# A decoder trunk's residual stream and FFN products kept token by token: tokens stationary, 512 weight columns moving

## The chip, the cores and the metric

The kernel runs on one core of a Trainium2 chip. The metric is the device time of one execution in microseconds; three runs were timed, and their median counts. The profile is of one further execution, read by the hardware profiler. TensorE (PE) multiplies matrices; VectorE (DVE), ScalarE (ACT) and GpSimd (POOL) work on elements; SyncE's queue (SP) issues the loads of the weights. Every engine works through its own list of instructions in order.

## The reference

Two layers act on x, 256 tokens of 1024 features. Each adds half of an FFN, a mixer, a cross-attention (xattn) into 256 memory tokens, and half of a second FFN. The mixer of layer 0 is a state-space head group with pooled channels; that of layer 1 is windowed attention with learned sinks. All is in float32.

```python
def rms_norm(x, gain):
    return x * lax.rsqrt(jnp.mean(x * x, axis=-1, keepdims=True) + EPS) * gain

def swiglu(h, wi, wo):                       # wi 1024 x 5632, wo 2816 x 1024
    gate, up = jnp.split(h @ wi, 2, axis=-1)
    return (jax.nn.silu(gate) * up) @ wo

for i in range(2):
    x = x + 0.5 * swiglu(rms_norm(x, ffn1_norm[i]), ffn1_wi[i], ffn1_wo[i])
    h = rms_norm(x, mix_norm[i])
    x = x + (ssd_pool_mixer(h, ...) if i == 0 else swa_sink_attention(h, ...))
    x = x + memory_cross_attention(rms_norm(x, xattn_norm[i]), mem_k, mem_v, xattn_wq[i], ...)
    x = x + 0.5 * swiglu(rms_norm(x, ffn2_norm[i]), ffn2_wi[i], ffn2_wo[i])
```

## The kernel before

A float32 product is done as three products of rounded parts (`mm3`, lines 165 to 167): hi by hi, lo by hi, hi by lo. Weights come in chunks, up to 1 MB each, through SP's queue into `raw`; ScalarE casts the hi part (`whi`, line 92) and VectorE subtracts the lo part (`wlo`, line 93), in pieces of 128 x 1024, five of which are held at a time. Taking a chunk starts the load and the split of the next one.

The residual stream `x` lies feature by feature: eight k tiles of 128 features by 256 tokens. In the FFN's two products, the q and output projections, a 128 x 128 tile of weights stays in TensorE and the 256 tokens move through it: a product is 128x256. Only the memory's and attention's keys and values (`token_mm`, line 936) and the last FFN's second product (`ffn_last`, line 509) have the tokens stay and 512 weight columns move: a product is 128x512.

When tile m of x is final, `x_ready` writes its scaled input for the next block at once: `h_hi` by ScalarE (274), `h_lo` by VectorE (275), its square (257) and the running sum `acc` (258). Behind the eighth tile, four passes of a product with ones add up the squares over the partitions (`stat`, 220), a chain of eleven small VectorE instructions makes rstd (`var` to `rcol`, 191 to 204 and 223), and another product spreads it over the partitions (`diag`, `rbc`, 228 and 237). What needs rstd is deferred until then, so the first products of a block run on the unscaled input. In the FFN, VectorE scales gate and up (`gu`, 441), ScalarE takes Silu (444), and `a_hi`, `a_lo` (446, 447) are the input of the second product.

TensorE's list is written in the order of the code. Small products, transposes among them, are put into it some tiles after the point that defers them: `LAGS` is the table, and `tick` counts four split products of 256 columns as one tile. On the other engines, instructions follow in the order of the program that a scheduler keeps.

The blocks in their order, with the layer as a number: FFN1_0, the memory's keys and values, mixer, xattn0, FFN2_0, FFN1_1, attention, xattn1, FFN2_1. "Border" below is the place in TensorE's list where one block's first large product follows the last of the block before.

Of the kernel before, what the change touches and what calls it, by code (L numbers as in the profile page):

```python
# [8 lines left out]
F32 = mybir.dt.float32  # L9
# [7 lines left out]
P = 128  # L17
# [9 lines left out]
# When the tensor engine's small products are issued: tiles (4 split products of 256 columns)  # L27
# after the point that defers them.
LAGS = {
    "sums": 6, "spread": 10, "first_keep": 2, "first_sums": 3, "first_spread": 7, "memT": 16, "kT": 12,  # L30
    "steps": 2, "decays": 14, "seg": [19, 21, 23, 24, 26, 49, 52, 54],
    "weigh": [25, 26, 27, 29, 31, 51, 57, 59], "cbt": 8, "pool": 9, "group_sums": 6, "group_spread": 15,
    "last": 2, "keys": 6, "xsT": [9, 13, 17, 20], "heads": [13, 16, 19, 22, 29, 34, 40, 46],
    "x_norm": [8, 11, 15, 17], "x_scores": [11, 12, 16, 20], "x_weights": [12, 12, 16, 22],
# [5 lines left out]
    "x_sums": 6, "a_sums": 4, "a_spread": 8, "m_sums": 4, "m_spread": 7,  # L40
# [4 lines left out]
# columns of the constant array  # L45
# [17 lines left out]
class Trunk:  # L63
# [11 lines left out]
    # ------------------------------------------------------------ helpers  # L75
# [11 lines left out]
    def split(self, raw, a, b):  # L87
        """hi + lo parts of [P, a, b] weights."""
        nc = self.nc
        hi = self.wp.tile([P, a, b], F32R, tag="whi", name="whi")  # L90
        lo = self.wp.tile([P, a, b], F32R, tag="wlo", name="wlo")
        nc.scalar.copy(hi, raw)  # L92
        nc.vector.tensor_tensor(out=lo, in0=raw, in1=hi.bitcast(F32), op=ALU.subtract)  # L93
        return hi, lo

    # The weights' chunks are listed in the order of their use; taking one starts the next one's
    # load and split.
    def plan(self, src, ka, cols, step):
        self.chunks.append((src, ka, cols, step))
# [5 lines left out]
    def load_chunk(self, by_part=False):  # L105
# [3 lines left out]
        src = src.rearrange("(k p) c -> p k c", p=P)  # L109
        if by_part:  # L110
            loads = [lambda k=slice(u, min(u + step, ka)): self.nc.sync.dma_start(
                out=raw[:, k, :], in_=src[:, k, :]) for u in range(0, ka, step)]
        else:
            self.nc.sync.dma_start(out=raw, in_=src)
# [18 lines left out]
    # Small products of the tensor engine are put between the large ones, some tiles after what  # L133
    # they wait for was started (LAGS).
# [4 lines left out]
    def tick(self, n=1):  # L139
# [3 lines left out]
        if self.count < 4:  # L143
            return
        self.count -= 4
        self.now += 1
# [98 lines left out]
    def warm(self, func):  # L245
        """has the scalar engine's table for func loaded."""
# [13 lines left out]
    def x_ready(self, m, gain):  # L260
        """x tile m is final for this block: its part of the next block's scaled input and norm."""
        nc = self.nc
        if gain is None:
            return
        xm = self.x[:, m, :]
        if m == 0:
            self.acc = self.sp.tile([P, NT], F32, tag="acc", name="acc")
        if gain[2]:
            self.square_into(self.acc, xm, m == 0)
            if m == KT - 1:  # L270
                self.normalised(gain)
            return
        g = self.col(gain[0], 8 * gain[1] + m)
        nc.scalar.activation(self.h_hi[:, m, :], xm, AF.Identity, scale=g)
        nc.vector.scalar_tensor_tensor(out=self.h_lo[:, m, :], in0=xm, scalar=g,
                                       in1=self.h_hi[:, m, :].bitcast(F32), op0=ALU.mult, op1=ALU.subtract)
        self.square_into(self.acc, xm, m == 0)
        if m == KT - 1:
            name = {"xattn_norm": "x_", "mix_norm": "a_"}.get(gain[0], "")
            self.block_rstd(self.acc, name, gain[0] != "xattn_norm")  # L280

    def block_rstd(self, acc, name="", wide=True):
# [3 lines left out]
        def done():  # L286
# [3 lines left out]
        self.R, self.RB = self.rstd(acc, D, self.sp, "rbx", name, done, wide)  # L290
# [7 lines left out]
    def normalised(self, gain):  # L298
        """the next block's input, normalised before its products."""
        nc = self.nc  # L300

        def scale():
            for m in range(KT):
                t = self.sp.tile([P, NT], F32, tag="xn", name="xn", bufs=3)
                nc.vector.scalar_tensor_tensor(out=t, in0=self.x[:, m, :],
                                               scalar=self.col(gain[0], 8 * gain[1] + m), in1=rb,
                                               op0=ALU.mult, op1=ALU.mult)
# [1023 lines left out]
```

## Time and profile before

| | |
|---|---|
| three runs | 1199.64, 1200.95, 1201.68 us |
| median | 1200.95 us |
| span of the profiled execution | 1198.2 us |
| the profiled execution's own time | not recorded beside the span; it is a fourth execution, not one of the three |
| TensorE busy | 1185.6 us, 99% |
| VectorE, ScalarE, GpSimd busy | 826.8, 666.6, 27.7 us |
| moved by DMA | 204.00 MB, 170 GB/s in the mean |

A busy time counts an instruction from its start to its end. Products of TensorE overlap: one of 256 columns lasts 0.28 us, but the next starts long before that. How long one holds up the next is read from starts that follow each other. In the list of groups, the idle time after the bar is that of the engine just before such an instruction, with what ended it.

### The profile page before, as it was taken

The page shows a single profiled execution, that of the slowest core. Times are in us where ns is not written, and L with a number is a line of the kernel's source. Part 1 is how long each engine was busy: PE and PEld are TensorE (multiplying, and loading weights), DVE is VectorE, ACT ScalarE, POOL GpSimd, SP SyncE. Part 2 cuts the span into 40 slices and gives each one's busy share as a digit, 9 for nine tenths or more (in the row PEclk, how much of TensorE's full clock was granted, in tenths as well). Part 3 has the DMA queues.
Part 4 walks back from the last instruction along what each step waited for, and adds up shares of the span by engine and source line. Part 5 has one row for each costly group of instructions (what it writes and reads, how often), then busy time and mean ns, then how long its engine had stood idle before and what let it go on. Part 6 is the DMA issues. An engine that isn't in the chain of part 4 may idle for free.

```text
span 1198.2 us, 22743 instructions
## 1 busy us (share of the span) xinstructions
PE 1185.6 (99%) x9351; PEld 1147.7 (96%) x9351; DVE 826.8 (69%) x1558; ACT 666.6 (56%) x1109; POOL 27.7 (2%) x45
## 2 busy tenths in 40 slices
PE   8999999999999999999999999999999999999998
PEld 8999999889999999999999999999988999999987
DVE  6767655879888786766655766665797877676642
ACT  7446444876775566544544544544478665554541
POOL 2000000000000000000000000000410000000000
PEclk9999999999999999999999999999999999999999
DMA  8564655554455534556465556455622434554651
GB/s 293 177 211 142 207 186 166 198 175 143 141 176 176 185 107 141 175 178 200 149 208 185 175 176 204 157 191 187 208 97 85 162 121 141 176 185 167 210 186 61
DMA packets 178231, 204.00 MB, mean 170 GB/s; under 512 B 4630, under 2 KB 162592, under 8 KB 178128
## 3 DMA queue, kind: packets, MB, share of 16 engines
q1 hardware_dynamic: 176512, 201.93, 51.2%
q8 instruction: 73, 1.20, 0.4%
q10 hardware_dynamic: 1040, 0.32, 0.1%
q0 software_dynamic: 576, 0.31, 0.1%
q14 instruction: 30, 0.25, 0.1%
HBM read 201.50 MB, written 1.05 MB: 169 GB/s over the span
## 4 chain that ended last, share of the span: by engine, by line
PE 96%; DVE 1%; ACT 1%; DMA 0%; issue 0%; SPq 0%; DVEq 0%
PE mmb L165 27%; PE mmb L166 26%; PE mmb L167 26%; PE mmb L509 5%; PE mmb L936 5%; PE oT L1219 0%; DMA xn<-in_x_dram 0%; PE pT L1207 0%; PE yps L651 0%; DVE wlo L93 0%; PE rbc L237 0%; ACT s L1188 0%; PE sc L1164 0%; PE pT L1015 0%; PE seg L552 0%
## 5 line engine op out<-in xcount | busy, mean ns | idle before, releaser
L93 DVE TENSOR_TENSOR wlo<-raw,whi 128x1024 fp32r<-128x1024 f32 (+1 forms) x385 | 462.4, 1204 | 182.1 <-ACT whi L92 180.9
L92 ACT CAST whi<-raw 128x1024 fp32r<-128x1024 f32 (+1 forms) x385 | 396.9, 1035 | 255.3 <-PE mmb L166 197.5
L165 PE MATMUL mmb<-h_hi,whi 128*128 128x256 f32 x1824 | 521.3, 286 | 1.4 <-ACT whi L92 1.4
L167 PE MATMUL mmb<-h_hi,wlo 128*128 128x256 f32 x1824 | 517.2, 284 | 1.7 <-DVE wlo L93 1.7
L166 PE MATMUL mmb<-h_lo,whi 128*128 128x256 f32 x1824 | 517.0, 283 | 0.0
L165 PEld LDWEIGHTS mmb<-h_hi,whi 128*128 128x128 f32 x1824 | 350.7, 192 | 4.5 <-issue 2.4
L167 PEld LDWEIGHTS mmb<-h_hi,wlo 128*128 128x128 f32 x1824 | 350.6, 192 | 2.1 <-DVE wlo L93 2.1
L166 PEld LDWEIGHTS mmb<-h_lo,whi 128*128 128x128 f32 x1824 | 350.8, 192 | 0.1
L167 PE MATMUL mmb<-a_hi,wlo 128*128 128x256 f32 x528 | 149.2, 283 | 0.0
L165 PE MATMUL mmb<-a_hi,whi 128*128 128x256 f32 x528 | 149.0, 282 | 0.0
L166 PE MATMUL mmb<-a_lo,whi 128*128 128x256 f32 x528 | 148.7, 282 | 0.0
L441 DVE TENSOR_TENSOR gu<-mmb,rb 128x512 f32<-128x512 f32 x88 | 60.2, 687 | 74.7 <-PE mmb L167 72.3
L444 ACT ACTIVATE s<-gu 128x256 f32<-128x256 f32 x88 | 36.4, 417 | 135.2 <-DVE gu L441 134.8
L166 PEld LDWEIGHTS mmb<-a_lo,whi 128*128 128x128 f32 x528 | 100.7, 191 | 0.0
L165 PEld LDWEIGHTS mmb<-a_hi,whi 128*128 128x128 f32 x528 | 100.7, 191 | 0.0
L167 PEld LDWEIGHTS mmb<-a_hi,wlo 128*128 128x128 f32 x528 | 100.6, 191 | 0.0
L446 ACT CAST a_hi<-s 128x256 fp32r<-128x256 f32 x88 | 35.3, 404 | 37.5 <-DVE s L445 37.5
L445 DVE TENSOR_TENSOR s<-s,gu 128x256 f32<-128x256 f32 x88 | 36.8, 421 | 19.8 <-ACT s L444 19.7
L447 DVE TENSOR_TENSOR a_lo<-s,a_hi 128x256 fp32r<-128x256 f32 x88 | 36.8, 421 | 17.0 <-ACT a_hi L446 17.0
L166 PE MATMUL mmb<-o_lo,whi 128*128 128x256 f32 x128 | 36.4, 284 | 2.0 <-DVE o_lo L1034 2.0
L165 PE MATMUL mmb<-o_hi,whi 128*128 128x256 f32 x128 | 36.6, 286 | 0.0
L167 PE MATMUL mmb<-o_hi,wlo 128*128 128x256 f32 x128 | 36.2, 283 | 0.0
(321 smaller groups left out, 1483.4 us busy)
## 6 DMA issues: line engine op xcount, KB each, us to landing
raw<-in_ffn_wi_dram SPq DMA_DIRECT2D x86, 1024.0 KB, 5.2
raw<-in_ffn_wo_dram SPq DMA_DIRECT2D x34, 1024.0 KB, 5.3
raw<-in_ssd_in_proj_dram SPq DMA_DIRECT2D x14, 1024.0 KB, 5.2
raw<-in_ffn_wo_dram SPq DMA_DIRECT2D x12, 768.0 KB, 4.6
raw<-in_mem_wkv_dram SPq DMA_DIRECT2D x8, 1024.0 KB, 5.2
raw<-in_even_out_proj_dram SPq DMA_DIRECT2D x8, 1024.0 KB, 5.1
raw<-in_xattn_wq_dram SPq DMA_DIRECT2D x8, 1024.0 KB, 5.1
raw<-in_xattn_wo_dram SPq DMA_DIRECT2D x8, 1024.0 KB, 5.0
```

The costliest lines, as they stand in the source:

```text
L92: nc.scalar.copy(hi, raw)
L93: nc.vector.tensor_tensor(out=lo, in0=raw, in1=hi.bitcast(F32), op=ALU.subtract)
L165: mm(ps, lhsT=wh, rhs=xh, start=start, stop=False, skip_group_check=True)
L166: mm(ps, lhsT=wh, rhs=xl, start=False, stop=False, skip_group_check=True)
L167: mm(ps, lhsT=wl, rhs=xh, start=False, stop=stop, skip_group_check=True)
L441: nc.vector.tensor_tensor(out=gu, in0=bank.rearrange("p (a n) -> p a n", a=2), in1=self.RB[:, None, :].to_broadcast([P, 2, NT]), op=ALU.mult)
L444: nc.scalar.activation(s, gu[:, 0, :], AF.Silu)
L445: nc.vector.tensor_tensor(out=s, in0=s, in1=gu[:, 1, :], op=ALU.mult)
L446: nc.scalar.copy(a_hi[:, f, :], s)
L447: nc.vector.tensor_tensor(out=a_lo[:, f, :], in0=s, in1=a_hi[:, f, :].bitcast(F32), op=ALU.subtract)
L509: nc.tensor.matmul(banks[b], lhsT=l[:, f, tok], rhs=r, start=f == 0 and i == 0, stop=f == NFF - 1 and i == 2)
L936: self.nc.tensor.matmul(ps, lhsT=l[:, f, tok], rhs=r, start=f == 0 and i == 0, stop=f == KT - 1 and i == 2)
```

## The change

`x` now lies token by token: two blocks of 128 tokens by 1024 features. `tok3` keeps 128 tokens in TensorE and moves 512 weight columns; both FFN products, the mixer's, xattn's and attention's output projections use it. q projections and the mixer's input projections still move 256 tokens.

`add_rows` adds 128 x 512 of a result to x, and ScalarE squares that and sums it by token at once (`square`). `half_ready` runs when 512 features of x are final: it puts two transposes for each of the four k tiles into TensorE's list (`turn_in`), behind which `put` writes `h_hi` and `h_lo` from PSUM; behind the second half, `token_rstd` makes rstd as a column. Only attention needs it over the partitions (`spread_rstd`). In the FFN, gate and up are scaled by the column; the product `s` is transposed (`gT`) before the second product. `tick` now counts in quarters of a tile. Chunks of the FFN's weights are 4 k tiles by 512 columns in place of 8 by 256. The two first heads of xattn are computed k tile by k tile.

```diff
 LAGS = {
-    "sums": 6, "spread": 10, "first_keep": 2, "first_sums": 3, "first_spread": 7, "memT": 16, "kT": 12,
+    "gT": 3, "hT": 1.5, "hT_soon": 1, "mT": 3.5, "memT": 16, "kT": 12,
...
+    def tok3(self, ps, x, w, start, stop):
+        mm = self.nc.tensor.matmul
+        (xh, xl), (wh, wl) = x, w
+        mm(ps, lhsT=xh, rhs=wh, start=start, stop=False)
+        mm(ps, lhsT=xl, rhs=wh, start=False, stop=False)
+        mm(ps, lhsT=xh, rhs=wl, start=False, stop=stop)
+        self.tick(2)
...
-    def x_ready(self, m, gain):
...
+    def add_rows(self, ps, b, c, scale=None):
+        xs = self.x[:, b, c * 512:(c + 1) * 512]
+        if scale is None:
+            self.nc.vector.tensor_tensor(out=xs, in0=ps, in1=xs, op=ALU.add)
...
+        self.square(b, c)
+    def square(self, b, c):
...
+        self.nc.scalar.activation(junk, self.x[:, b, c * 512:(c + 1) * 512], AF.Square,
+                                  accum_out=self.ss[:, b, c:c + 1])
+    def half_ready(self, c, gain, lag="hT"):
+        if gain[2]:
+            if c == 1:
+                self.token_rstd()
+                self.normalised(gain)
             return
+        for k in range(4):
+            self.turn_in(self.x, 4 * c + k, gain, LAGS[lag] + k)
+        if c == 1:
+            self.token_rstd()
+            if gain[0] == "mix_norm":
+                self.spread_rstd()
+    def turn_in(self, src, k, gain, lag):
...
+            self.nc.tensor.transpose(ps[:, b * P:(b + 1) * P], src[:, b, k * P:(k + 1) * P], self.idn)
+            if b == 1:
+                self.put(self.h_hi[:, k, :], self.h_lo[:, k, :], ps, g)
+        for b in range(2):
+            self.tasks.append((self.now + lag + b / 2, lambda b=b: turn(b)))
...
     def ffn(self, gain, early=None):
...
+            def columns():
                 banks = [self.bank(), self.bank()]
+                for k0 in (0, 4):
+                    self.rows_mm(banks, self.take(), 4, k0, self.hk, KT)
+                return banks
+            def turn(s, f, i, b, st):
...
+                nc.tensor.transpose(ps[:, i * NT + b * P:i * NT + (b + 1) * P],
+                                    s[b][:, (f + i) % 4 * P:((f + i) % 4 + 1) * P], self.idn)
+                if (i, b) == (1, 1):
...
+            for j in range(6):
+                n = 512 if j < 5 else 256
...
+                gate = columns()
+                for b in range(2):
+                    nc.scalar.activation(s[b][:, :n], gate[b][:, :n], AF.Silu, scale=self.R[:, b:b + 1])
+                up = columns() if j < 5 else gate
...
+            for c in range(2):
                 banks = [self.bank(), self.bank()]
+                for k0 in range(0, NFF, 4):
+                    self.rows_mm(banks, self.take(), min(4, NFF - k0), k0,
+                                 lambda f: (a_hi[:, f, :], a_lo[:, f, :]), NFF)
...
+                        self.add_rows(banks[b], b, c, 0.5)
+                if gain:
+                    self.half_ready(c, gain)
+    def rows_mm(self, banks, w, kn, k0, kk, last):
+        for k in range(kn):
+            xh, xl = kk(k0 + k)
+            for b in range(2):
+                tok = slice(b * P, (b + 1) * P)
+                self.tok3(banks[b], (xh[:, tok], xl[:, tok]), w(k, 0, 512), k0 + k == 0, k0 + k == last - 1)
...
+        for c in range(2):
+            for b in range(2):
+                tok = slice(b * P, (b + 1) * P)
+                for k in range(2):
+                    xh, xl = kk(6 + k)
+                    self.tok3(banks[c][b], (xh[:, tok], xl[:, tok]), w(k, c * 512, 512), False, k == 1)
+                self.add_rows(banks[c][b], b, c)
+            self.half_ready(c, gain, "hT" if c else "hT_soon")
```

Three places show how the lists move. The first is VectorE's list at the border from xattn0 to FFN2_0; x is the residual stream, h_lo the next block's input, wlo a piece of its weights. Before:

```order
L93 TENSOR_TENSOR wlo<-raw,whi 128x1024
L781 TENSOR_TENSOR x<-mmb,x 128x256 x3
L275 SCALAR_TENSOR_TENSOR h_lo<-x,cols_181,h_hi 128x256
L781 TENSOR_TENSOR x<-mmb,x 128x256
L275 SCALAR_TENSOR_TENSOR h_lo<-x,cols_181,h_hi 128x256
L258 TENSOR_TENSOR acc<-acc,sq 128x256
```

After the change, at the same border:

```order
L279 TENSOR_TENSOR x<-mmb,x 128x512 x4
L93 TENSOR_TENSOR wlo<-raw,whi 128x1024
L857 SCALAR_TENSOR_TENSOR h_lo<-hT,cols_198,h_hi 128x256
L327 TENSOR_TENSOR var<-ss 128x2
L328 TENSOR_SCALAR var<-var 128x2
L93 TENSOR_TENSOR wlo<-raw,whi 128x1024
L205 TENSOR_SCALAR rst<-var 128x2
L857 SCALAR_TENSOR_TENSOR h_lo<-hT,cols_198,h_hi 128x256
```

The first h_lo stood behind three additions of 256 columns and stands behind four of 512 and a split; the second one has a further split and the head of the rstd chain ahead of it.

The second is ScalarE's list at the same border; o_hi is the last head's output, h_hi the next block's input. Before:

```order
L1033 CAST o_hi<-oT 128x512
L92 CAST whi<-raw 128x1024
L274 ACTIVATE h_hi<-x,cols_181 128x256
L254 ACTIVATE acc<-x 128x256
L274 ACTIVATE h_hi<-x,cols_181 128x256
```

After the change (`junk,ss` is the square with its sum by token):

```order
L1055 CAST o_hi<-oT 128x512
L92 CAST whi<-raw 128x1024
L289 ACTIVATE junk,ss<-x 128x512 x2
L92 CAST whi<-raw 128x1024
L289 ACTIVATE junk,ss<-x 128x512
L856 ACTIVATE h_hi<-hT,cols_198 128x256
L289 ACTIVATE junk,ss<-x 128x512
L92 CAST whi<-raw 128x1024
```

Three squares and a second split now stand ahead of the first h_hi.

The third is TensorE's list where attention takes rstd spread over the partitions; hT is a transposed tile of x. Before, behind the last of 48 products for keys and values:

```order
L936 MATMUL mmb<-whi,h_hi 128x512
L936 MATMUL mmb<-whi,h_lo 128x512
L936 MATMUL mmb<-wlo,h_hi 128x512
L237 MATMUL rbc<-diag,ones 128x128 x2
L165 MATMUL mmb<-h_hi,whi 128x256
```

After the change:

```order
L960 MATMUL mmb<-whi,h_hi 128x512
L960 MATMUL mmb<-whi,h_lo 128x512
L960 MATMUL mmb<-wlo,h_hi 128x512
L316 MATMUL hT<-idn,x 128x128
L344 MATMUL rbc<-diag,ones 128x128 x2
L960 MATMUL mmb<-whi,h_hi 128x512
```

The spreading product stood behind 48 products of the block; it stands behind 18 of them and four transposes.

## Rows read from the trace of the kernel before

**Rows 1.** The page: busy time, share and instructions; the chain that ended last.
```profile
PE 1185.6 (99%) x9351; PEld 1147.7 (96%) x9351; DVE 826.8 (69%) x1558; ACT 666.6 (56%) x1109; POOL 27.7 (2%) x45
PE 96%; DVE 1%; ACT 1%; DMA 0%; issue 0%; SPq 0%; DVEq 0%
```
**Rows 2.** Busy us by stretch: stretch and length, then PE, PEld, DVE, ACT, POOL, PEclk, DMA.
```profile
417.00:484.00 67.00, 65.98 (x553) 65.58 (x553) 51.29 (x149) 40.67 (x76) 0.00 (x0) 1.00 0.40 133
484.00:860.00 376.00, 376.00 (x3113) 374.91 (x3111) 236.87 (x330) 185.88 (x259) 6.02 (x5) 1.00 0.56 183
```
**Rows 3.** TensorE's waits: what ended them, us in total, times, longest.
```profile
PE mmb L166 <- DVE o_lo L1034: 2.0, 2, 1.0
PE mmb L167 <- DVE wlo L93: 1.7, 2, 0.9
```
**Rows 4.** Timeline of TensorE: start us, us, line, operation, [idle before], at xattn0's end.
```profile
471.47 0.28 PE L165 MATMUL mmb<-h_hi,whi 128*128 128x256 f32 x1
...
474.35 0.28 PE L165 MATMUL mmb<-h_hi,whi 128*128 128x256 f32 x1
```
**Rows 5.** The chain that ended last, in order of time: start us, us, what.
```profile
1145.66 49.01 PE mmb L509 x216
```
**Rows 6.** Timeline of TensorE around four transposes in the last block.
```profile
1141.85 0.60 PE L492 MATMUL xN<-idn,x 128*128 128x128 f32 x4
1142.20 0.48 PE L509 MATMUL mmb<-whi,a_hi 128*128 128x512 f32 x1
1142.52 0.40 PE L509 MATMUL mmb<-whi,a_lo 128*128 128x512 f32 x1
1142.75 0.40 PE L509 MATMUL mmb<-wlo,a_hi 128*128 128x512 f32 x1
1142.98 0.40 PE L509 MATMUL mmb<-whi,a_hi 128*128 128x512 f32 x1
1143.22 0.39 PE L509 MATMUL mmb<-whi,a_lo 128*128 128x512 f32 x1
```
**Rows 7.** Timeline of TensorE around one group for the statistics.
```profile
211.15 0.50 PE L220 MATMUL stat<-ones,acc 128*128 128x1 f32 x4
...
211.82 0.39 PE L936 MATMUL mmb<-whi,t_lo 128*128 128x512 f32 x1
```
**Rows 8.** Timeline of VectorE at xattn0's end.
```profile
468.01 1.20 DVE L781 TENSOR_TENSOR x<-mmb,x 128x256 f32<-128x256 f32 x3
469.13 0.48 DVE L275 SCALAR_TENSOR_TENSOR h_lo<-x,cols,h_hi 128x256 fp32r<-128x256 f32 x1
469.53 0.41 DVE L781 TENSOR_TENSOR x<-mmb,x 128x256 f32<-128x256 f32 x1
469.86 0.48 DVE L275 SCALAR_TENSOR_TENSOR h_lo<-x,cols,h_hi 128x256 fp32r<-128x256 f32 x1
```
**Rows 9.** VectorE's groups by line and shape: busy us, mean ns | idle before.
```profile
L93 DVE TENSOR_TENSOR wlo<-raw,whi 128x1024 fp32r<-128x1024 f32 x373 | 454.1, 1221 | 179.1 <-ACT whi L92 177.9 <-ACT a_hi L446 0.3
L441 DVE TENSOR_TENSOR gu<-mmb,rb 128x512 f32<-128x512 f32 x88 | 60.2, 687 | 74.7 <-PE mmb L167 72.3 <-ACT rb L239 2.3
L275 DVE SCALAR_TENSOR_TENSOR h_lo<-x,cols,h_hi 128x256 fp32r<-128x256 f32 x48 | 23.1, 483 | 0.0
```
**Rows 10.** ScalarE's groups by line and shape.
```profile
L92 ACT CAST whi<-raw 128x1024 fp32r<-128x1024 f32 x373 | 389.4, 1048 | 249.1 <-PE mmb L166 191.5 <-PE mmb L509 23.9 <-issue 13.1
L963 ACT ACTIVATE qsq<-mmb 128x512 f32<-128x512 f32 x8 | 4.7, 593 | 0.3 <-PE mmb L167 0.2
L397 ACT ACTIVATE h_hi<-xT,cols 128x256 fp32r<-128x256 f32 x8 | 3.5, 480 | 4.4 <-PE xT L392 4.4
L1000 ACT ACTIVATION_READ_ACCUMULATOR p<-sc,mx,rsy 128x1 f32 x16 | 3.1, 197 | 0.0
```
**Rows 11.** Timeline of VectorE through one rstd chain.
```profile
480.84 0.14 DVE L223 TENSOR_SCALAR var<-stat 128x2 f32<-128x2 f32 x1
...
483.00 0.48 DVE L228 TENSOR_SCALAR diag<-idn,rcol 128x128 f32<-128x128 f32 x2
```

More of the change, by code (lines that the diff above doesn't have):

```diff
@@ L98, in plan @@
     def plan(self, src, ka, cols, step):
-        self.chunks.append((src, ka, cols, step))
+        self.chunks.append((src if isinstance(src, list) else [src], ka, cols, step))
     def start_chunk(self):
@@ L142, in tick @@
         self.count += n
[L143 to L146, printed above, removed]
+        self.now = self.count / 4
         self.run_tasks(lambda due: due <= self.now)
@@ new lines, in token_rstd, with spread_rstd, spread @@
+    def token_rstd(self):
+        nc = self.nc
+        self.R = self.sp.tile([P, 2], F32, tag="rcol", name="rcol")
+        v = self.sp.tile([P, 2], F32, tag="var", name="var")
+        nc.vector.tensor_tensor(out=v, in0=self.ss[:, :, 0], in1=self.ss[:, :, 1], op=ALU.add)
+        nc.vector.tensor_scalar(out=v, in0=v, scalar1=1.0 / D, scalar2=EPS, op0=ALU.mult, op1=ALU.add)
+        self.rsqrt(v, 2, self.R)
+    def spread_rstd(self):
+        nc = self.nc
+        self.waiting = []
+        self.RB = self.sp.tile([P, NT], F32, tag="rbx", name="rb", bufs=1)
+        dg = self.sp.tile([P, 2, P], F32, tag="diag", name="diag", bufs=1)
+        for b in range(2):
+            nc.vector.tensor_scalar(out=dg[:, b, :], in0=self.idn, scalar1=self.R[:, b:b + 1],
+                                    scalar2=None, op0=ALU.mult)
+        def spread():
+            bc = self.abank("rbc")
+            for b in range(2):
+                nc.tensor.matmul(bc[:, b * P:(b + 1) * P], lhsT=self.ones, rhs=dg[:, b, :],
+                                 start=True, stop=True)
+            nc.scalar.copy(self.RB, bc[:, :NT])
@@ L289, in done @@
                 fn()
-        self.R, self.RB = self.rstd(acc, D, self.sp, "rbx", name, done, wide)
+        self.defer("a_spread", spread)
     def normed(self, fn):
@@ L298, in normalised @@
     def normalised(self, gain):
[L300 to L307, printed above, removed]
-                nc.scalar.copy(self.h_hi[:, m, :], t)
-                nc.vector.tensor_tensor(out=self.h_lo[:, m, :], in0=t, in1=self.h_hi[:, m, :].bitcast(F32),
-                                        op=ALU.subtract)
-        _, rb = self.rstd(self.acc, D, self.sp, "rbx", "m_", scale)
+        xs = self.memp.tile([P, 2, D], F32, name="xs")
+        for c in range(2):
+            for b in range(2):
+                cc = slice(c * 512, (c + 1) * 512)
+                self.nc.vector.tensor_scalar(out=xs[:, b, cc], in0=self.x[:, b, cc], scalar1=self.R[:, b:b + 1],
+                                             scalar2=None, op0=ALU.mult)
+        for k in range(KT):
+            self.turn_in(xs, k, gain, LAGS["mT"] + k)
     def setup(self):
@@ L377, in col, with first_input @@
         return self.cols[gi][:, at + i:at + i + 1]
-    def first_input(self, xn):
-        nc = self.nc
-        banks = []
+    def first_input(self):
         loads, parts = zip(*(self.load_chunk(True) for _ in range(2)))
-        for u in range(2):
-            for load in loads:
+        for load in loads:
+            for u in range(2):
                 load[u]()
@@ L397, in first_input @@
-                nc.scalar.activation(self.h_hi[:, m, :], src, AF.Identity, scale=g)
-                nc.vector.scalar_tensor_tensor(out=self.h_lo[:, m, :], in0=src, scalar=g,
-                                               in1=self.h_hi[:, m, :].bitcast(F32),
-                                               op0=ALU.mult, op1=ALU.subtract)
-            if q < 2:
-                parts[q][0]()
-        for p in parts:
-            p[1]()
-        acc = self.sp.tile([P, 2], F32, tag="acc0", name="acc0", bufs=1)
@@ new lines, in first_input, with plan_ffn @@
+            parts[q // 2][q % 2]()
+        for b in range(2):
+            for c in range(2):
+                self.square(b, c)
+        self.token_rstd()
+    def plan_ffn(self, wi, wo):
+        for j in range(5):
+            for t in (0, DFF):
+                for k0 in (0, 4):
+                    self.plan(wi[k0 * P:(k0 + 4) * P, t + j * 512:t + (j + 1) * 512], 4, 512, 2)
+        for k0 in (0, 4):
+            rows = wi[k0 * P:(k0 + 4) * P, :]
+            self.plan([rows[:, 2560:DFF], rows[:, DFF + 2560:]], 4, 512, 2)
+        for c in range(2):
+            for k0 in range(0, NFF, 4):
+                kn = min(4, NFF - k0)
+                self.plan(wo[k0 * P:(k0 + kn) * P, c * 512:(c + 1) * 512], kn, 512, 2)
@@ L1233, in attention @@
                     self.token_mm(banks[b], wk[k // 4], (k % 4, k % 4 + 1), k // 4 * 4, self.h_hi, self.h_lo, b)
-            self.normed(keys_values)
+            keys_values()
+            for b in range(2):
+                nc.gpsimd.tensor_tensor(out=self.x[:, b, :], in0=self.x[:, b, :], in1=bo, op=ALU.add)
             for f in range(8):
```

277 lines of the change are left out of this document (109 added, 168 removed).

## Prediction, made before the run

> **What bounds the kernel now.** I read the page's busy shares and its chain first [rows 1]: TensorE is busy for 1185.6 of 1198.2 us and the chain that ended last is 96% TensorE, so whatever makes that engine's list shorter shortens the run, and whatever makes it wait lengthens it. The table by stage [rows 2] says where it waits already: from 484 to 860 us, through the end of one FFN, the border to the next and that one too, not at all (376.00 of 376.00), at the xattn about 1.0 us. The largest waits by line [rows 3] are 2.0 us, twice 1.0, on o_lo and 1.7 on a piece of weights. VectorE (69%) and ScalarE (56%) are no bound by their totals. What they can cost is order: both work through one list, and a product waits for what stands late in it.
>
> Two slots follow, each from the start of one product to the start of the next (durations overlap and are no use here). 256 columns: 24 products start between 471.47 and 474.35 us [rows 4], 0.1200 us each. 512 columns: 216 products take 49.01 us [rows 5], 0.2269 us each. One 512-column product replaces two of 256, so a pair saves 0.0131 us.
>
> Beside that row stands a rule. The Trainium skill (TensorE: Matmul & The Clock Gate, "Wait — 56ns, not 53.3ns?") gives the warm spacing as N / 2.4 GHz plus about 2.5 ns per matmul, which would be 109 and 216 ns; the rows disagree, with some 13 ns over the columns' time at both widths. By the page's figure a pair would save 2.5 ns only, and this change's saving would be an estimated 8.5 us in place of 44.4 us. The sum below goes by the rows.
>
> **The change on TensorE.** Counted in the order of both kernels:
> - 6768 products of 256 columns go, 3384 of 512 come: 6768 x 0.1200 = 812.2, 3384 x 0.2269 = 767.8, saving 44.4 us. If only 0.1190 holds for the old slot the saving is 37.5 us.
> - 288 transposes come (176 of the FFN activations, 112 of x), 16 of the last block go. Before, a group of four stands between 512-column products [rows 6]: from 1141.85 to the second product after it at 1142.52 is 0.67 us, less one product slot 0.443, or 0.111 each. The products after it start 0.233 apart (1142.52 to 1143.22, three), 0.006 over the steady slot. The new ones stand alone, mostly one after every third product, so each may also carry three such products' excess: 0.130. I take 0.122, between the two: 288 x 0.122 = 35.1 us (32.0 to 37.4), less 16 x 0.111 = 1.8.
> - 7 groups for the statistics and 5 that spread rstd over the partitions go. One costs 211.15 to 211.82 less a product slot, 0.44 us [rows 7]; the spreading ones, as many passes, I price the same: 12 x 0.44 = 5.3 us.
>
> TensorE's list: -44.4 + 35.1 - 1.8 - 5.3 = -16.4 us; with both bad ends -7.2, with the good end of the transposes -19.5.
>
> Other parts cost nothing in the steady stretches. The weights' volume, their splits and loads stay (385 splits against 379); four FFNs have two more half-loads in SP's queue, beside transfers that fill half of the time [rows 2]. In the FFN the scaled product, Silu and the put of two transposed tiles leave VectorE and ScalarE less to do than gu, s, a_hi and a_lo did, and the transpose waits three tiles of 1.36 us behind the last product, against some 2 us of work. The bias addition is two POOL instructions, off the path while the attention runs. At the start four squares stand behind the first puts; I take 0, ends -1 and +1 us. The two o_lo waits stay.
>
> **The change at the borders.** This is the cost. Before, a border is covered: xattn0's output tiles end one by one, h_lo of k=0 is there at 469.61 and of k=1 at 470.34 [rows 8], while the next block's first product starts at 471.47 [rows 4]. Now x is ready in halves of 512 columns, a k tile has to be transposed behind it, and the order puts splits, squares and the rstd chain between the puts. Durations used: split 1.05 on ScalarE and 1.22 on VectorE, put 0.48 on each, an addition like L441 0.69 [rows 9, 10], a square of 512 columns 0.59 and its accumulator 0.20 [rows 10]. The chain from var to rcol takes 2.16 us for eleven instructions, 0.20 each, and the two diag 0.48 [rows 11]. A 512-column product lasts 0.39 us of which its slot is 0.23 [rows 6], so its result is there 0.16 us after the slot.
>
> *xattn to FFN2*, t=0 where the next block would begin. ScalarE: a split freed by TensorE at -1.0 ends at 0.05, the third square at 0.84, then h_hi(0) at 1.32: TensorE waits 1.32. VectorE: fourth addition to 0.73, split to 1.95, h_lo(0) to 2.43 where 1.55 was due: 0.88 more. Then the last square (2.11), three small ones, a split whose whi is there at 3.16 (to 4.4), one more, h_lo(1) at 5.1; due at 4.05: 1.05. Eight small ones and h_lo(2) at 7.2, due 6.85: 0.35. One more split and h_lo(3) at 9.2, due 8.95: 0.25. Sum 3.85 us. From k=4 the puts are ahead. This border is there twice; attention to xattn1 has the same lists under 256-column products, 1.44 us a k tile, and comes to 4.0.
>
> *FFN1_1 to attention*: additions to 0.9, a split to 2.1, squares to 2.25, ten small ones to 4.25, split to 5.45, one small, h_lo(4) to 6.1, one small, h_lo(5) to 6.8, diag to 7.25. TensorE reaches the spreading product behind 18 products and four transposes, at 4.6: it waits 2.65 us, and behind it stand all products of the block.
>
> *FFN2_0 to FFN1_1*: the same lists without diag. h_lo(4) at 6.1 is due at 6.4: nothing. *FFN1_0 to memory*: the transposes of xs wait for R (5.65) and two scalings, 6.3 against 4.8: 1.5. *Mixer to xattn0*: h_lo(6) stands behind two splits, of which the second waits for a buffer that TensorE gives back at 6.3: about 9.1 against 8.0, 1.1.
>
> Sum: 2 x 3.85 + 4.0 + 2.65 + 0 + 1.5 + 1.1 = 16.95 us. No row before shows these waits; the nearest, o_lo behind its ScalarE half, is 1.0 us [rows 3]. From below the bound is 2.65, the one wait that no later put can hide, from above half as much again, 25.
>
> **Sum.** -16.4 + 17.0 = +0.6 us on the profiled execution. It spans 1198.2 us, the runs shown read 1199.64 to 1201.68 with median 1200.95, 2.75 above the span, which I carry unchanged: 1201.5 us.
>
> **Rivals.**
> - *The list gain shows, the borders are mostly covered.* For it: VectorE sits idle before its splits for a long time, waiting on ScalarE, so a split may be done long before its place in my reckoning; before, no border loses anything. Against: the lists are in order and the squares stand in them. Then only 2.65 stays: 1200.95 - 16.4 + 2.65 = 1187 us.
> - *A late border feeds itself (slower).* ScalarE's splits wait for buffers that TensorE releases. Where TensorE waits for a put, the release behind it is late, so the next split, which stands ahead of the next put on both engines, is late too. At the three xattn borders three splits lie between the puts; if each is exposed for its 1.22 us beyond my sums, 3 x 3 x 1.22 = 11 us: 1212.5. It decides from the point where a split's release comes after the put that TensorE waits for; in my lists that is so only at k=3, hence not my forecast.
> - *The wide product saves almost nothing.* If 512-column products in the FFN, whose stationary tiles change with every product as in the rows, started every 0.2375 us, close to two narrow ones at 0.2400, TensorE's list would take 3384 x 0.2375 = 803.7 in place of 767.8 us, 36 us more: 1237. That is what the page's 2.5 ns named above would make of it. The row of the same operation [rows 5] says 0.2269, so almost nothing is left for it.
> - That the change doesn't do what it says is excluded: its order has 3888 products of 512 columns and 1512 of 256.
>
> **How the numbers follow.** Under 0.2% (2.4 us) either way a measurement of this kernel can't tell from no change. The balance (1201.5, own range 1195 to 1208) has 0.50: 0.16 of it faster, 0.25 within, 0.09 slower. The covered borders have 0.26, all faster; the self-feeding border 0.22 and the page's rule 0.02, slower. So faster 0.42, same 0.25, slower 0.33. The range reaches from the covered case to the self-feeding one, 1187 to 1212.5: about 0.1 beyond each end.
>
> **What would show it.** Products of 512 columns at L182 every 0.227 us and a lone transpose adding 0.11 to 0.13; waits of TensorE on h_hi and h_lo (L856, L857) at the three xattn borders, 3 to 4 us each, the first of them on ScalarE; one wait of 2 to 3 us at the spreading product L344; none between FFN2_0 and FFN1_1. The lists' theory is wrong if those waits stay under 5 us together, the stream's if the 512-column slot in the FFN is over 0.232 or a transpose costs over 0.15. Then the sign follows the one that failed.

## The result, and the profile after

The changed kernel takes 1217.35 us (median of four runs, 1216.99 to 1218.75). The kernel before took 1200.41 us on the same chip (1199.64 to 1201.68). The ratio is 1.0139, 95% interval 1.0124 to 1.0153: slower by 17 us, outside the forecast range. The spans of the profiled executions, 1215.4 and 1198.2 us, differ by 17.2 us.

The page's busy row, to be held against [rows 1]:

```profile
PE 1187.9 (98%) x6191; PEld 986.2 (81%) x6191; DVE 751.7 (62%) x1295; ACT 649.1 (53%) x1012; POOL 30.9 (3%) x46
```

VectorE and ScalarE work less, TensorE is busy 2.3 us longer and 15 us more of the span it is not busy. Its longer waits by line, which answer to [rows 3] (what ended them, us in total, times, longest; dots mark lines left out):

```profile
PE mmb L171 <- DVE h_lo L857: 3.0, 3, 1.1
PE mmb L182 <- DVE h_lo L857: 2.8, 4, 0.7
PE rbc L344 <- DVE diag L338: 2.5, 1, 2.5
PE mmb L181 <- ACT h_hi L856: 2.0, 2, 1.0
...
PE kT L1131 <- DVE kd L1155: 1.4, 2, 1.1
...
PE hT L316 <- DVE xs L364: 1.2, 1, 1.2
PE pT L1037 <- ACT p L1030: 1.1, 1, 1.1
...
PE mmb L170 <- ACT h_hi L856: 1.0, 1, 1.0
```

The waits on h_hi and h_lo are those of the borders, rbc is the spreading product. The border from xattn0 to FFN2_0 in TensorE's timeline (start us, us, line, operation, idle before), where [rows 4] had no wait at all:

```profile
471.14 0.27 PE L316 MATMUL hT<-idn,x 128*128 128x128 f32 x1
472.39 0.49 PE L181 MATMUL mmb<-whi,h_hi 128*128 128x512 f32 x1 [0.98 <-ACT h_hi L856]
473.62 0.78 PE L182 MATMUL mmb<-whi,h_lo 128*128 128x512 f32 x1 [0.73 <-DVE h_lo L857]
474.19 0.63 PE L183 MATMUL mmb<-wlo,h_hi 128*128 128x512 f32 x1
474.62 0.42 PE L316 MATMUL hT<-idn,x 128*128 128x128 f32 x1
474.69 0.78 PE L181 MATMUL mmb<-whi,h_hi 128*128 128x512 f32 x1
475.26 0.63 PE L182 MATMUL mmb<-whi,h_lo 128*128 128x512 f32 x1
475.69 0.63 PE L183 MATMUL mmb<-wlo,h_hi 128*128 128x512 f32 x1
...
481.40 0.51 PE L182 MATMUL mmb<-whi,h_lo 128*128 128x512 f32 x1 [0.69 <-DVE h_lo L857]
```

Beside the three waits the reader is to see the starts from 474.19 to 475.69: 0.43 us or more from product to product, about twice the steady slot. The table by stretch shows why (columns as in [rows 2]; PEclk, the granted clock, is the third last number):

```profile
473.70:477.10 3.40, 3.40 (x9) 2.61 (x10) 2.78 (x10) 0.66 (x2) 0.00 (x0) 0.50 0.75 243
```

The clock is granted at 0.50, the lower of its two levels (1.2 of 2.4 GHz), for 3.4 us. TensorE had just stood still twice, with one product between. The same happens at 951.5 and 1019.8 us, behind the two other borders of this kind. In the kernel before it happened once, from 13.7 to 17.2 us, behind the waits of the start.

VectorE's list at that border, to be held against [rows 8]:

```profile
471.34 0.69 DVE L279 TENSOR_TENSOR x<-mmb,x 128x512 f32<-128x512 f32 x1 [0.92 <-PE mmb L183]
471.95 1.22 DVE L93 TENSOR_TENSOR wlo<-raw,whi 128x1024 fp32r<-128x1024 f32 x1
473.08 0.48 DVE L857 SCALAR_TENSOR_TENSOR h_lo<-hT,cols,h_hi 128x256 fp32r<-128x256 f32 x1
473.48 0.15 DVE L327 TENSOR_TENSOR var<-ss 128x2 f32<-128x2 f32 x1
473.66 0.17 DVE L328 TENSOR_SCALAR var<-var 128x2 f32<-128x2 f32 x1
473.92 1.23 DVE L93 TENSOR_TENSOR wlo<-raw,whi 128x1024 fp32r<-128x1024 f32 x1
```

h_lo stands behind the last addition and a split: the list of the forecast, in its order.

The steady stretches hold what no wait shows. First, 20 products' starts in FFN2_0's first matrix, with h stationary; then 30 in its second, with a:

```profile
519.80 0.39 PE L182 MATMUL mmb<-whi,h_lo 128*128 128x512 f32 x1
...
524.33 0.39 PE L181 MATMUL mmb<-whi,h_hi 128*128 128x512 f32 x1
...
651.61 0.40 PE L182 MATMUL mmb<-whi,a_lo 128*128 128x512 f32 x1
...
658.61 0.40 PE L182 MATMUL mmb<-whi,a_lo 128*128 128x512 f32 x1
```

4.53 / 20 = 0.2265 us against 7.00 / 30 = 0.2333 us, for the same instruction shape. Over all steady stretches the mean is 0.2268 with h, 0.2333 with a, between 0.2323 and 0.2336 with o, p, ao, t and y. A lone transpose (gT) among products with h:

```profile
552.42 0.27 PE L490 MATMUL gT<-idn,s 128*128 128x128 f32 x1
552.45 0.47 PE L181 MATMUL mmb<-whi,h_hi 128*128 128x512 f32 x1
552.76 0.39 PE L182 MATMUL mmb<-whi,h_lo 128*128 128x512 f32 x1
552.99 0.39 PE L183 MATMUL mmb<-wlo,h_hi 128*128 128x512 f32 x1
...
554.03 0.27 PE L490 MATMUL gT<-idn,s 128*128 128x128 f32 x1
```

Two transposes with six products take 1.61 us, 0.805 for each transpose with its three products; less three slots of 0.2267 the transpose costs 0.125.

**Account of the 17.2 us**, from starts that follow each other in TensorE's timeline. Waits: 26.8 us after, 10.0 before (0.3 us or more of excess over the usual distance, without those at the low clock), so +16.8. Low clock: three falls against one, each 3.4 us at half speed, 1.7 lost, so +3.4. The rest, TensorE's list itself, is 17.2 - 16.8 - 3.4 = -3.0 where -16.4 was forecast. The figure of the waits, and with it this rest, moves by half a microsecond with the bound above which an excess is counted as a wait.

### The profile page after: what moved, and what is told of

It reads as the page before. It is cut to its first block, busy times and chain, and to the rows that moved or that the text cites. A ratio compares the mean times of both kernels' runs of the same rounds, so it can differ in the third digit from the quotient of the medians.

```text
span 1215.4 us, 16052 instructions
## 1 busy us (share of the span) xinstructions
PE 1187.9 (98%) x6191; PEld 986.2 (81%) x6191; DVE 751.7 (62%) x1295; ACT 649.1 (53%) x1012; POOL 30.9 (3%) x46
## 3 DMA queue, kind: packets, MB, share of 16 engines
HBM read 202.02 MB, written 1.05 MB: 167 GB/s over the span
## 5 line engine op out<-in xcount | busy, mean ns | idle before, releaser
L93 DVE TENSOR_TENSOR wlo<-raw,whi 128x1024 fp32r<-128x1024 f32 x379 | 463.2, 1224 | 389.8 <-ACT whi L92 387.0
L92 ACT CAST whi<-raw 128x1024 fp32r<-128x1024 f32 x379 | 397.3, 1050 | 431.9 <-PE mmb L182 389.8
L181 PE MATMUL mmb<-whi,h_hi 128*128 128x512 f32 x704 | 292.6, 416 | 3.6 <-ACT h_hi L856 2.0
L182 PE MATMUL mmb<-whi,h_lo 128*128 128x512 f32 x704 | 276.6, 393 | 2.8 <-DVE h_lo L857 2.8
L183 PE MATMUL mmb<-wlo,h_hi 128*128 128x512 f32 x704 | 276.3, 392 | 0.6 <-DVE wlo L93 0.6
L170 PE MATMUL mmb<-h_hi,whi 128*128 128x256 f32 x416 | 122.5, 294 | 1.0 <-ACT h_hi L856 1.0
L171 PE MATMUL mmb<-h_lo,whi 128*128 128x256 f32 x416 | 118.7, 285 | 3.0 <-DVE h_lo L857 3.0
L172 PE MATMUL mmb<-h_hi,wlo 128*128 128x256 f32 x416 | 118.1, 284 | 0.0
L171 PEld LDWEIGHTS mmb<-h_lo,whi 128*128 128x128 f32 x416 | 80.1, 193 | 4.1 <-DVE h_lo L857 3.8
L170 PEld LDWEIGHTS mmb<-h_hi,whi 128*128 128x128 f32 x416 | 79.9, 192 | 4.2 <-issue 2.4
```

Of the source, the lines that this page charges most:

```text
L170: mm(ps, lhsT=wh, rhs=xh, start=start, stop=False, skip_group_check=True)
L171: mm(ps, lhsT=wh, rhs=xl, start=False, stop=False, skip_group_check=True)
L172: mm(ps, lhsT=wl, rhs=xh, start=False, stop=stop, skip_group_check=True)
L181: mm(ps, lhsT=xh, rhs=wh, start=start, stop=False)
L182: mm(ps, lhsT=xl, rhs=wh, start=False, stop=False)
L183: mm(ps, lhsT=xh, rhs=wl, start=False, stop=stop)
```

## The experiments

Three questions were open: why the 512-column slot has two values, whether the border waits are paid in full, and whether a wait that is taken away goes or moves on. The kernel before was timed beside each set of runs, with medians from 1200.45 to 1201.51 us, so a difference of 1 us between runs of different sets says nothing.

**The operands' places.** In each kernel all pieces of the weights lie at one place modulo 256 bytes of a partition: at 128 in the kernel before, at 96 after. In the kernel before, h, a (but for FFN1_0), o, p and t lie at the same place modulo 256: distance 0. After the change the pool of small tiles, which lies ahead of these, has another size; a, o, p, ao and t are 32 bytes off, a of FFN1_0 64, y 128, and h, in the pool right behind the weights, still 0. (The addresses are those that the built programs carry; a distance below is the activation's start less the weights', modulo 256.) `align` puts all back to 0 by three unused tiles:

```diff
+        self.sp.tile([P, 56], F32, name="pad", bufs=1)
...
+            if early:
+                ap.tile([P, 56], F32, name="pada")
...
+                    kp.tile([P, 40], F32, name="pady")
```

> After the change, 512-column products start every 0.2267 us where the stationary tile is h_hi/h_lo and every 0.2333 us where it is a, p, o, t or y. In SBUF, h lies a multiple of 256 bytes from the weight pieces that move, the others do not (a, p, o, t by 32 bytes more, y by 128, the first FFN's a by 64). This kernel adds unused tiles (224 bytes per partition in the small pool, 224 in the first FFN, 160 before y), so that all stationary tiles lie a multiple of 256 bytes from the moving pieces; no instruction changes. Address theory: every wide product starts every 0.227 us; 1056 products of the second FFN matrices, 480 of the output projections and 192 of the memory, 1728 x 0.0066 = 11.4 us less, about 1206 us. Rival, that other engines' traffic or the accumulators set the slot: no change, 1217 us, slot in the second FFN matrix still 0.233.

Measured: 1207.75 us, ratio to before 1.0062 (1.0045 to 1.0079), 9.6 us under the changed kernel. The same 30 products as above:

```profile
651.71 0.39 PE L182 MATMUL mmb<-whi,a_hi 128*128 128x512 f32 x1
...
658.51 0.39 PE L182 MATMUL mmb<-whi,a_hi 128*128 128x512 f32 x1
```

6.80 / 30 = 0.2267. Nothing but addresses differs, so the slot follows the operands' places. It is not a's own place that counts: outside FFN1_0 a lies at 128 modulo 256 in both kernels, and its wide products start every 0.227 us before (weights at 128, [rows 5]) and every 0.2333 after (weights at 96). Two more versions of the changed kernel, `sweep1` and `sweep2`, set another distance in each FFN by the size of an unused tile before a_hi. `sweep1`:

```diff
+            self.nth = getattr(self, "nth", -1) + 1
+            if (8, 56, 24, 8)[self.nth]:
+                ap.tile([P, (8, 56, 24, 8)[self.nth]], F32, name="pada")
```

(`sweep2` takes 24, 40, 48 and 56.)

> As after the change, with unused tiles ahead of the FFN's a_hi, another width for each FFN, so that its distance from the moving weight pieces, modulo 256 bytes, is 96 in FFN1_0, 0 in FFN2_0, 128 in FFN1_1 and 64 in FFN2_1. Read: the slot of the 512-column products in each second matrix. Address theory: 0.2267 us in FFN2_0 and 0.2333 us in FFN1_0; FFN1_1 tells whether 128 bytes suffice, FFN2_1 whether 64 do. Rival: 0.2333 us in all.

> The changed kernel with unused tiles ahead of a: distance modulo 256 bytes 160 in FFN1_0, 192 in FFN2_0, 224 in FFN1_1, 0 in FFN2_1. Address theory: 0.2267 us in FFN2_1 alone, 0.232 to 0.235 in the other three. Rival, that the place of the block counts: FFN2_1 stays at 0.2333.

And the kernel before, where the weights are stationary and 256 columns of the activation move: `before_off32` sets h, a, o, p, ao and y 32 bytes off the weights and leaves t, and the a of the last FFN, at 0; `sweepb` sets four other distances in the FFNs.

```diff
+        self.xp.tile([P, 8], F32, name="padx")
...
+            if gain is None:
+                ap.tile([P, 56], F32, name="pada")
...
+                    kp.tile([P, 40], F32, name="pady")
...
+        mp.tile([P, 56], F32, name="padt")
```

> The kernel before, with unused tiles only: h, p, o, ao, y and a, which move through the 256-column products, lie 32 bytes more than a multiple of 256 from the stationary weight pieces; t and the last FFN's a stay at a multiple for their 512-column products. In the profile of the kernel before, the first FFN's a lies 32 bytes off and its 528 products start every 0.1178 us; all others, at 0, every 0.1200. Address theory, which says that the distance of the two operands in SBUF sets the slot of narrow products too: 8280 - 528 products x 0.0022 = 17 us less, 1184 us. Rival, that the first FFN's slot has another cause (its place in the program, fewer transfers): 1201 us.

> The kernel before with unused tiles ahead of the FFN's a: its distance from the weight pieces, modulo 256 bytes, is 64 in FFN1_0, 224 in FFN2_0 and 160 in FFN1_1 (256-column products, a moves) and 192 in FFN2_1 (512-column products, a stays). Address theory: the slots of the second matrices differ from 0.1200 where the distance favours them, FFN1_0 is no longer at 0.1178 as at 32, and FFN2_1 is at 0.233. Rival: 0.1178 in FFN1_0 and 0.1200 in the other two, 0.2269 in FFN2_1, as before.

Measured: `before_off32` 1178.72 us, ratio 0.9816 (0.9798 to 0.9834), faster than both kernels. 24 of its products, where [rows 4] has 2.88 us:

```profile
559.57 0.28 PE L167 MATMUL mmb<-h_hi,wlo 128*128 128x256 f32 x1
...
562.37 0.28 PE L167 MATMUL mmb<-h_hi,wlo 128*128 128x256 f32 x1
```

2.80 / 24 = 0.1167 us in place of 0.1200. Some 7400 narrow products went from distance 0 to 32: 7400 x 0.0033 = 24 us, and 21.7 went (1200.45 to 1178.72); in its trace the clock, of which more below, was low for 10.2 us before the last product in place of 3.4. The expectation had the direction, but 17 us, since it went by the 0.1178 of FFN1_0. `sweep1` took 1218.37, `sweep2` 1214.13 and `sweepb` 1197.96 us, one run each. The slots by distance, means over some 240 to 528 products of an FFN's second matrix (192 where y is named), in ns:

| distance | 512 columns move, activation stationary | 256 columns move, weights stationary |
|---|---|---|
| 0 | 226.7 | 120.0 |
| 32 | 233.3 | 116.7; 117.8 in FFN1_0 of before and for y |
| 64 | 233.3 | 117.8 |
| 96 | 234.3 | 120.0 (y) |
| 128 | 232.5 | not measured |
| 160 | 233.3 | 117.3 |
| 192 | 228.9 | not measured |
| 224 | 233.3 | 118.3 |

So the wide form wants distance 0, and the narrow one is as slow there as at any distance measured. Two expected values did not come: 192 gives the wide form 228.9, not 232 or more, and at 64 FFN1_0 keeps its 117.8 in the narrow form. Why the distance acts, and why 32 gives two values in the narrow form, stays open: the a of FFN1_0 has the same place and the same distance modulo 256 in `before` and `before_off32`, and takes 117.8 and 116.7. So the distance modulo 256 is not all that sets the narrow slot.

**Is the spreading product's wait paid?** `spread6` moves it three tiles later:

```diff
-    "a_spread": 3,
+    "a_spread": 6,
```

> The product that spreads rstd over the partitions in attention stands 6 tiles behind the last product in place of 3; nothing else moves. Order theory: the 2.64 us wait at 861 us goes, and nothing that is late follows, since the puts behind it are done by then: 1214.7 us. Rival, that the wait only moves on to the next late put: under 1 us gained, 1216.5 us or more.

Measured: 1216.69 us, ratio 1.0129 (1.0113 to 1.0144), 0.7 us under the changed kernel, whose own runs spread over 1.8. The figure is the rival's, its mechanism only in part:

```profile
PE kT L1131 <- DVE kd L1155: 2.5, 1, 2.5
```

rbc no longer waits; the keys' transposes, which TensorE now reaches sooner, wait 2.5 us for kd, which VectorE has no earlier (1.4 in two waits before this edit). So 1.1 of the 2.5 us moved on, and the rest was gained there. But behind that wait the clock is low (columns as in [rows 2]):

```profile
880.50:887.30 6.80, 6.80 (x36) 5.96 (x35) 5.27 (x21) 2.78 (x5) 0.00 (x0) 0.50 0.42 154
```

6.8 us at 0.50 cost 3.4 us, and the changed kernel has no fall in its attention: in this trace the clock took the gain away. Whether such a fall comes differs between executions: the four took 1213.97 to 1218.33 us, at a mean granted clock of 0.998 and 0.993.

**The order at the border.** `late_rstd` lets the second half's squares and the rstd chain be issued behind the last put, at the borders into both xattns and both second FFNs:

```diff
+        late = gain[0] in ("ffn2_norm", "xattn_norm") and c == 1
+        if not late:
+            for b in range(2):
+                self.square(b, c)
...
+            with self.tc.issue_after(hi):
+                for b in range(2):
+                    self.square(b, 1)
+            with self.tc.issue_after(lo):
+                self.token_rstd()
```

> At the borders into both xattns and into both second FFNs, the squares of the second half of x and the rstd chain are issued behind the last put of h; nothing else changes. Order theory: one square ahead of the first h_hi and the small instructions ahead of the second and third h_lo go; each of the three borders behind an output projection loses 1 to 1.5 us of its 3.1 to 3.6 us of waiting, 1213 us. Rival, that the splits in the lists are what holds the puts: under 0.5 us a border, 1216 us or more; the granted clock still falls to 0.5 there.

Measured: 1214.56 us, ratio 1.0113 (1.0098 to 1.0128), 2.8 us under the changed kernel. The border in its timeline:

```profile
473.66 0.50 PE L181 MATMUL mmb<-whi,h_hi 128*128 128x512 f32 x1 [0.37 <-ACT h_hi L873]
474.36 0.50 PE L182 MATMUL mmb<-whi,h_lo 128*128 128x512 f32 x1 [0.20 <-DVE h_lo L874]
474.70 0.40 PE L183 MATMUL mmb<-wlo,h_hi 128*128 128x512 f32 x1
...
477.03 0.50 PE L182 MATMUL mmb<-whi,h_lo 128*128 128x512 f32 x1 [0.75 <-DVE h_lo L874]
```

The first two waits are halved, a third of 1.0 us appears at 477.03 and one stays at 481.7: 3.0 us together where 3.08 were. What stands ahead of the later puts now is splits. So neither theory came out whole: the waiting stayed, as the rival had it. But the clock no longer falls here: the products behind 474.70 start at their usual distance. It falls elsewhere in this trace, at 11.1, 437.7 and 861.0 us, as often as in the changed kernel, so this trace alone does not show that the clock is what gained. All traces together show where the falls come. With the first order (`after`, `align`, `spread6`, `sweep1`, `sweep2`) the clock falls behind 14 of the 15 borders of the three kinds above; with the later order (`late_rstd`, `align_late`, `combo`) behind none of 9. `align_late` joins this order with the places of `align`:

> The aligned version of the changed kernel with the later squares and rstd chain at the same borders (both edits were run alone: -9.6 us by the operands' places, -2.8 us by the order). If the two add up, 1207.75 - 2.8 = 1205.0 us, ratio to before 1.0038; if the order's gain was only the clock falling elsewhere by chance, 1207.0 to 1208.5, ratio 1.0055 to 1.0068.

Measured: 1204.78 us, ratio 1.0031 (1.0018 to 1.0044), 3.0 under `align`: in the median the two add up. Its trace has no fall of the clock before 1200 us, when the last products have ended; that of `align` has two, at 944.3 and 1012.6 us. Two falls cost 3.4 us, and the two spans differ by 3.3 (1205.6 and 1202.3), with the border waits as they were. So waits of the same sum cost less when they lie apart, in most executions: two of the five of `align_late` have a mean clock of 0.996, as three of the four of `align` do, and took 1206.14 and 1206.46 us against 1207.39 to 1207.91. `combo` adds to that two later places in the attention:

```diff
-    "keys": 6, "xsT": [9, 13, 17, 20], "heads": [13, 16, 19, 22, 29, 34, 40, 46],
+    "keys": 7, "xsT": [9, 13, 17, 20], "heads": [13, 16, 19, 22, 29, 34, 40, 46],
...
-    "a_spread": 3,
+    "a_spread": 5,
```

> The changed kernel with all stationary tiles at a multiple of 256 bytes from the moving pieces, the second half's squares and rstd behind the puts, the spreading product 5 tiles behind in place of 3 and the keys' transposes 7 in place of 6. If the three add up: 1217.35 - 9.6 (addresses) - 2.8 (late rstd) - 1.5 (attention) = 1203.5 us, still not faster than before, since some 16 us of border waits and clock falls are left against a gain of 16 on TensorE's list. Rival, that the alignment gain is partly lost to later waits: 1207 us.

Measured: 1210.26 us, ratio 1.0084 (1.0066 to 1.0102), a miss: 5.5 us over `align_late`. rbc and kT wait no more, and these do, with the clock low for 10 us in the attention:

```profile
PE qst L1203 <- ACT asq L1190: 4.9, 3, 3.6
...
PE sc L1219 <- DVE sm L1249: 1.9, 1, 1.9
...
PE pT L1263 <- DVE s L1257: 1.5, 1, 1.5
```

The stretches of low clock:

```profile
873.70:877.10 3.40, 3.40 (x18) 3.38 (x17) 1.98 (x12) 2.87 (x5) 0.00 (x0) 0.50 0.90 308
914.60:921.40 6.80, 6.79 (x22) 4.42 (x23) 5.36 (x16) 1.97 (x6) 0.00 (x0) 0.50 0.00 1
```

With one more fall, of 3.4 us at 433.3, the low clock costs 6.8 us here and nothing in `align_late`. The spans differ by 6.1 us (1208.4 and 1202.3), so nearly all of the loss is low clock, behind waits that the edit moved.

**The border itself.** `early_old_x` takes away what the border's puts wait for, on top of `align`:

```diff
+            if f0 == 0:
+                for k in range(KT):
+                    self.turn_in(self.x, k, gain, 1 + k)
...
-            self.half_ready(c, gain, "hT" if c else "hT_soon")
+            self.half_ready(c, gain, early=True)
```

> The aligned version of the changed kernel (1207.75 us, ratio to before 1.0062), with one thing else: at the three borders behind an output projection of 512 columns (xattn0 to FFN2_0, attention to xattn1, xattn1 to FFN2_1) the sixteen transposes for the next block's input and their puts are issued four tiles into the output projection instead of behind its end, and so read x before the block's own output is added to it. That addition is the part of the computation left out of the next block's input; every instruction stays. If the border waits and the falls of the clock right behind them are paid in full, the changed kernel's waits there (3.08 + 3.58 + 3.07 = 9.7 us) go, and with them up to 3.4 us of low clock: 1194.6 to 1198.0 us, ratio 0.995 to 0.998, and no wait on h_hi or h_lo at these borders. If the waits only move on (to the scaling by rstd, to the splits, to a_hi), under 3 us go: 1204.8 or more, ratio 1.004 or more. If the puts, now among the output projection's splits, delay the last additions, waits of 1 us appear inside the projection and a middle figure comes out.

Measured: 1193.98 us, ratio 0.9940 (0.9924 to 0.9957), 13.8 us under `align`, slightly more than the first theory gave. It leaves out the addition named, so it is a probe and no version of the kernel. The border is closed (compare 472.39 and 473.62 above):

```profile
468.87 0.39 PE L183 MATMUL mmb<-whi,o_lo 128*128 128x512 f32 x1
469.10 0.39 PE L184 MATMUL mmb<-wlo,o_hi 128*128 128x512 f32 x1
469.32 0.39 PE L182 MATMUL mmb<-whi,h_hi 128*128 128x512 f32 x1
469.55 0.39 PE L183 MATMUL mmb<-whi,h_lo 128*128 128x512 f32 x1
```

The spans differ by 13.2 us. Of these the three borders' waits in `align` are 3.5 + 3.6 + 3.1 = 10.2, one fall of the clock fewer is 1.7 (one is left, behind the rbc wait at 850 us), and the kT wait is 0.7 shorter; 0.6 us stay open. So the border waits do not move on. They are paid whole, with the clock on top.

## Why the prediction was wrong

**The step that failed: 3384 x 0.2269.** The 512-column slot was read from one stretch of one block [rows 5] and carried to all others. Of the changed kernel's 3888 such products, 1728 have a stationary operand off the weights' place, because the pool of small tiles between them has another size, and their steady slot is 0.2323 to 0.2336. At 0.2333 that would be 1728 x 0.0066 = 11.4 us. `align` gives back 9.6 in the medians; in the traces it is 9.8, of which 1.7 are one fall of the clock fewer, so the places themselves are worth some 8 us (6 of them from a, the rest from o, p, ao, t and y, which stand among more small instructions and gain less than their slots say). The prediction's own mark, a slot over 0.232 in the FFN, was passed. Two smaller terms belong to the list: the 528 narrow products of FFN1_0's second matrix ran at 0.1178 before, not at the 0.1200 of [rows 4] (1.2 us), and the transpose costs 0.125 among products with h, not 0.122 (at most 0.9 us). Of the 13.4 us that the list's -16.4 lacks, some 10 have a cause by this; what the other 3 are stays open. The second value of the narrow slot stood in the trace of before. It was a hint that a slot depends on more than the shape, and the prediction does not name it.

The rival "the wide product saves almost nothing" was given 0.02. For 1728 products the measured 0.2333 lies between its 0.2375 and the forecast's 0.2269, but not for its reason; for the others it was wrong. The Trainium skill (TensorE: Matmul & The Clock Gate, "Wait — 56ns, not 53.3ns?") puts some 2.5 ns per matmul over the columns' time. These runs do not agree at any distance: it is 10 ns at the least (0.1167 us for 256 columns, which alone are 106.7 ns at 2.4 GHz), and in the wide form 13 at distance 0 and 16 to 21 elsewhere.

**Low clock: a term that was missing.** +3.4 us. The forecast's border waits are counted as time lost and nothing else, but three of them were followed by 3.4 us at half speed. [rows 2] shows 1.00 throughout, in stretches where TensorE stood still for 1.0 us or not at all.

**The border term was right** by its places, and its sum came near: 15.05 us in place of 16.95.

| border | forecast us | measured us |
|---|---|---|
| xattn0 to FFN2_0 | 3.85 | 3.08 |
| xattn1 to FFN2_1 | 3.85 | 3.07 |
| attention to xattn1 | 4.0 | 3.58 |
| FFN1_1 to attention (rbc) | 2.65 | 2.64 |
| FFN2_0 to FFN1_1 | 0 | 0 |
| FFN1_0 to memory | 1.5 | 1.34 |
| mixer to xattn0 | 1.1 | 1.34 |

The waits named were found: on h_hi first, then on h_lo, and one at L344. The covered borders (1187) are refuted by the rows behind an output projection. Of the self-feeding border (1212.5) there is a trace: at k=3, the one place where its condition was reckoned to hold, h_lo at 481.40 is waited for 0.94 us where 0.25 was due. But k=1 and k=2, forecast at 1.05 and 0.35, do not wait, so the sum is smaller and not 3.7 us larger. Behind the first two waits of the border to FFN2_0, which were 2.14 us where 2.20 was forecast, the forecast had 1.65 us in three places and 0.94 came in one; that the sums are this close is in part luck. The time came nearer to 1212.5 than to the forecast by another road.

**Costs put at nothing.** The attention behind the late rbc: its own waits grew from 3.3 to 5.8 us, since kT now waits for kd, 1.2 us and 0.6. The first two heads of xattn, computed together: a new wait of 1.27 us on p (L1037). The start gained 1.2, and the two o_lo waits, kept at 2.4 in the forecast, are 1.6. Together with the borders, 15.05 + 2.5 + 1.3 - 1.2 - 0.8 = +16.8, the account's figure for the waits.

A small error went the other way: the 2.75 us carried from the span to the time is 1.8 in the changed kernel's profiled execution (1217.21 and 1215.4).

So the change is slower by two things, the operands' places (9.6 us by `align`, with one fall of the clock) and the three borders with their clock (13.8 by `early_old_x`); without both the time is 1193.98. The second was forecast but for the clock, the first was not. The places cut both ways: the kernel before, with its operands 32 bytes off, takes 1178.72 us. Against the best that these runs have of the change with all its work in it (1204.78), the narrow form is ahead by 26 us, and the 13.1 ns by which a wide product seemed to beat two narrow ones [rows 4, 5] are 2 x 116.7 - 226.7 = 6.7 ns when each lies at its best place.

## What to carry to other kernels

Before a slot is carried from one loop to another, look whether the trace has the same shape at a second speed, and print where both operands of the matmul lie: a tile that is added to or dropped from an unrelated pool can move them, and a few unused bytes put ahead of them are the cheapest experiment there is (9.6 us in one kernel, 21.7 in the other). A border wait on a fresh operand was paid whole here, and waits that follow each other closely may cost the clock as well: spreading them saved 3 us in the median with their sum unchanged. A wait that is taken away by a later place in the list is gone only if nothing behind it is late for a reason of its own; here that was kT, then qst. And before a gain or a loss of a few microseconds is put down to an edit, compare where the clock fell in the two traces: it hid the gain of `spread6` and made the loss of `combo`.

## What the runs showed of the hardware that was not expected

- The distance between a matmul's two operands, modulo 256 bytes of a partition, goes with its steady slot: 226.7 to 234.3 ns for 512 columns, 116.7 to 120.0 ns for 256. The two forms do not like the same distance, and in the narrow form one distance (32) has two values.
- The granted clock fell to 0.50 for some 3.4 us behind two waits of about 1.1 us with one product between (1.14 and 1.00 at the border shown), at 14 of 15 such borders in five traces. It did not fall behind waits of 0.53, 0.47, 1.02 and 0.99 us with more products between, at none of 9 such borders in three traces. In some traces it falls elsewhere, and the rbc wait of 2.5 us is followed by a fall in `late_rstd`, `sweep1` and `early_old_x` but not in `after`, `align` and `align_late`, so a single fall is no property of a line.
